# Short weight subtractions beside indirect writes, index products on VectorE, index copies on ScalarE, another pace of the list writes

## The chip, the cores and the metric

The kernel runs on one core of a Trainium2 chip. The metric is the device time of one execution in microseconds. Engines are called as in the profile: PE (TensorE), ACT (ScalarE), DVE (VectorE), POOL (GpSimd) and SP (the queue that issues most transfers).

## The reference, cut to what matters

Two transformer blocks over 256 tokens of width 2048. The stage that is changed is the feed-forward part of the first block, a retrieval over 16,384 one-neuron experts:

```python
q = einsum('td,de->te', ht, w_q)                          # 8 heads x 2 halves x 128
scores = einsum('thcd,hcnd->thcn', q, sub_keys)
s1, i1 = top_k(scores[:, :, 0], 16)
s2, i2 = top_k(scores[:, :, 1], 16)
cand_scores = s1[..., :, None] + s2[..., None, :]         # 16 x 16 for each head
cand_idx = i1[..., :, None] * 128 + i2[..., None, :]
top_scores, top_pos = top_k(cand_scores, 16)
experts = take_along_axis(cand_idx, top_pos)              # 128 experts for each token
gates = softmax(top_scores)
a = einsum('td,thkd->thk', x, u[experts])
out = einsum('thk,thkd->td', gates * gelu(a), v[experts])
```

## The kernel before

The tokens are two tiles (tt = 0 and 1) of 128. Every large product goes through PE in pieces: one piece is a weight block of 128 x 4 x 512 values, read into `raw` (3 buffers), copied by ACT into `whi` in a shorter format (L155), and the rest `wlo = raw - whi` taken by DVE (L156). PE then makes 24 matmuls of 512 columns (L180 to L182: hi x hi, hi x lo, lo x hi, for four rows of the block and two token tiles). `whi` and `wlo` have 3 buffers each, and `split(i + AHEAD)` with AHEAD = 2 stands ahead of the matmuls of piece i. So the split of piece i + 2 can start when PE has ended piece i - 1, and PE needs it when it comes to piece i + 2.

All other work is written as generators, in a list `tasks`. After the matmuls of each piece, `tick()` steps every generator once, in the order in which they were spawned. What a step issues stands in the engines' queues behind the split of that tick and ahead of the next one. Each queue is worked off in order, so a `yield` more or less moves all that follows by one piece. Nothing else orders the work.

The generators in this stage, in order of time:

- `peer_q(c)`, four chunks of four pieces (one per 512 columns of the query product), gives scores; `lists` takes the 16 best of 128 for each half head by `top16`: two maxima, two index searches, one replacement, and a cast of the indices from integers (L929).
- `route`, spawned ahead of all of them, works through the 8 heads of tile 0 and then of tile 1: candidates (L944), `top16` over 256, and for each pair of heads a position split into row and column (L954 to L957), one-hot masks (L960), their product with the index tables on POOL (L964), and a sum on DVE (L969). At its end come the softmax (its exponential on ACT, L974) and the expert numbers. `lists` for tile 1 is called from here. While tile 1 is routed, the gates of tile 0 are being written.
- `scatter_gates(tt)`: in each of 32 ticks DVE makes four comparisons (L1021), and POOL issues four indirect writes of 128 values each (L1006) into a table `gm` in memory, 128 writes for a tile. The table's 128 x 16,384 places say which expert has which gate. The next tile's writes start when those of the tile before are issued.
- `find_hits(tt)` reads the table back in 16 reads of 512 KB and reduces each (L1043); SP holds a read until all writes of the tile have landed.
- `list_experts` numbers the experts that were hit and issues 128 more indirect writes (`ls`, L1006); then SP reads the list back (L1136) and DVE copies it (L1139). With it the second half, `expert_v`, gathers its rows.

Meanwhile PE goes through the 32 chunks of `expert_u`, four pieces each; after the first piece of a chunk it transposes the chunk before (L235, eight transposes), ACT applies gelu to them (L1156), and ahead of that ACT has emptied the accumulators (L1150). Eight pieces of `mem_kv` follow, then 111 pieces of `expert_v`.

Of the kernel before, what the change touches and what calls it, by code (L numbers as in the profile page):

```python
# [8 lines left out]
F = mybir.dt.float32  # L9
# [5 lines left out]
OP = mybir.AluOpType  # L15
# [23 lines left out]
def tile_kernel(ctx, tc, a, o):  # L39
# [11 lines left out]
    def new(shape, dt=F, cls=None):  # L51
        n = 4 if dt != B16 else 2
        for s in shape[1:]:
            n *= s
        if cls is None:
            cls = next(c for c in SIZES if SIZES[c] >= n)
        uid[0] += 1
        return ar.tile(list(shape), dt, tag=cls, bufs=SLOTS[cls], name=f"{cls}_{uid[0]}")
# [32 lines left out]
    def spawn(gen):  # L91
        t = Task(gen)
        tasks.append(t)
        return t
# [32 lines left out]
    def load_raw(i):  # L127

        if i < len(srcs):
# [14 lines left out]
                    load(t[:, k], ap[:, k])  # L144
            raws[i] = t

    def split(i):
        if i < len(srcs):
            kt, n = srcs[i][1:3]
            live[home(i)].remove(i)  # L150
            r = raws.pop(i)
            hi = wp.tile([P, kt, n], R, tag="whi", bufs=SPLIT_BUFS, name=f"whi{i}")
            lo = wp.tile([P, kt, n], R, tag="wlo", bufs=SPLIT_BUFS, name=f"wlo{i}")
            for k in parts(i, kt):
                S.copy(hi[:, k], r[:, k])  # L155
                V.tensor_sub(lo[:, k], r[:, k], hi[:, k].bitcast(F))  # L156
            splits[i] = (hi, lo)

    def nxt():
# [754 lines left out]
    def lists(c, tt, sc):  # L914
        for b in range(4):
            top16(slot["s"][:, tt, 4 * c + b], slot["i"][:, tt, 4 * c + b], sc[:, b], P)
            if b % 2:
                yield

    def top16(val, idx, src, n):  # L920

        iu = new([P, 16], U32)
        rest = new([P, n])
        V.max(val[:, 0:8], src)
        V.max_index(iu[:, 0:8], val[:, 0:8], src)
        V.match_replace(rest, val[:, 0:8], src, -3.0e38)
        V.max(val[:, 8:16], rest)
        V.max_index(iu[:, 8:16], val[:, 8:16], rest)
        V.tensor_copy(idx, iu)  # L929

    def route():

        for tt in range(2):
            s, ix = slot["s"][:, tt], slot["i"][:, tt]
            ts, tp = new([P, 8, 16]), new([P, 8, 16])
            hi, lo = new([P, 8, 16]), new([P, 8, 16])
            i16 = st["iota"][:, :16]
            for h in range(8):
                while ("pq", h // 2) not in st or not st["pq", h // 2].done:
                    yield  # L940
                if tt and h % 2 == 0:
                    yield from lists(h // 2, 1, st["scores", h // 4][:, h // 2 % 2])
                cand = new([P, 16, 16])
                V.tensor_tensor(cand, s[:, 2 * h].unsqueeze(2).to_broadcast([P, 16, 16]),  # L944
                                s[:, 2 * h + 1].unsqueeze(1).to_broadcast([P, 16, 16]), op=OP.add)
                top16(ts[:, h], tp[:, h], cand.rearrange("p a b -> p (a b)"), 256)
                if tt:
                    yield
                if h % 2 == 0:
                    yield  # L950
                    continue

                h0, hs = h - 1, slice(h - 1, h + 1)
                V.tensor_scalar(hi[:, hs], tp[:, hs], 1.0 / 16, -0.46875, op0=OP.mult, op1=OP.add)  # L954
                V.tensor_scalar(hi[:, hs], hi[:, hs], 12582912.0, None, op0=OP.add)
                V.tensor_scalar(hi[:, hs], hi[:, hs], 12582912.0, None, op0=OP.subtract)
                V.scalar_tensor_tensor(lo[:, hs], hi[:, hs], -16.0, tp[:, hs], op0=OP.mult, op1=OP.add)  # L957
                eqs = [new([P, 2, 16, 16], cls="k2") for _ in range(2)]
                for eq, sel in zip(eqs, (hi, lo)):
                    V.tensor_tensor(eq, sel[:, hs].unsqueeze(3).to_broadcast([P, 2, 16, 16]),  # L960
                                    i16.unsqueeze(1).unsqueeze(1).to_broadcast([P, 2, 16, 16]), op=OP.is_equal)
                src = ix.rearrange("p (h c) k -> p h c k", c=2)[:, hs]
                for which, eq in enumerate(eqs):
                    G.tensor_tensor(eq, eq, src[:, :, which].unsqueeze(2).to_broadcast([P, 2, 16, 16]), op=OP.mult)  # L964
                yield
                if tt:
                    yield
                for eq, nm in zip(eqs, ("i1", "i2")):
                    V.tensor_reduce(slot[nm][:, tt, 16 * h0:16 * h0 + 32].rearrange("p (h k) -> p h k", h=2), eq,  # L969
                                    axis=AX.X, op=OP.add)  # L970
            nm8, sm = new([P, 8]), new([P, 8])
            V.tensor_scalar(nm8, ts[:, :, 0], -1.0, None, op0=OP.mult)
            V.tensor_tensor(ts, ts, nm8.unsqueeze(2).to_broadcast([P, 8, 16]), op=OP.add)
            S.activation(ts, ts, AF.Exp)  # L974
            V.tensor_reduce(sm, ts, axis=AX.X, op=OP.add)
            V.reciprocal(sm, sm)
            V.tensor_tensor(slot["gt"][:, tt].rearrange("p (h k) -> p h k", h=8), ts,
                            sm.unsqueeze(2).to_broadcast([P, 8, 16]), op=OP.mult)
            if tt == 0:
                slot["ex"], slot["au"] = new([P, 2, 2, P]), new([P, 2, P], U32)  # L980
            ex, au, ad = slot["ex"][:, tt, 0], slot["au"][:, tt], new([P, P])
            V.scalar_tensor_tensor(ex, slot["i1"][:, tt], float(P), slot["i2"][:, tt], op0=OP.mult, op1=OP.add)
            V.tensor_scalar(ad, ex, float(P), st["token"], op0=OP.mult, op1=OP.add)


            eh, ah = (x.rearrange("p (h k) -> p h k", h=8) for x in (ex, ad))
            eq, twice = new([P, 7, 7, 7], cls="k2"), new([P, 7, 7])
            V.tensor_tensor(eq, eh[:, 1:8, 0:7].unsqueeze(3).to_broadcast([P, 7, 7, 7]),
                            eh[:, 0:7, 9:16].unsqueeze(2).to_broadcast([P, 7, 7, 7]), op=OP.is_equal)
            V.tensor_reduce(twice, eq, axis=AX.X, op=OP.max)  # L990
            V.scalar_tensor_tensor(ah[:, 1:8, 0:7], twice, float(1 << 22), ah[:, 1:8, 0:7], op0=OP.mult, op1=OP.add)
            V.tensor_copy(au, ad)
            st["scatter", tt] = spawn(scatter_gates(tt, ex, au, slot["ex"][:, tt, 1]))
            yield
        while not st["scatter", 1].done:
            yield
        st["list"] = spawn(list_experts())
# [15 lines left out]
    def scatter_gates(tt, ex, au, total):  # L1013

        while tt and not st["scatter", 0].done:
            yield
        gt, group = slot["gt"][:, tt], []
        for k0 in range(0, P, 4):
            for k in range(k0, k0 + 4):
                same = new([P, P])  # L1020
                V.scalar_tensor_tensor(same, ex, ex[:, k:k + 1], gt, op0=OP.is_equal, op1=OP.mult, accum_out=total[:, k:k + 1])  # L1021
            for k in range(k0, k0 + 4):
                group.append(scatter("gates%d" % tt, gm[tt], au[:, k:k + 1], total[:, k:k + 1], group[k - 8:k - 7] if k >= 8 else ()))
            yield
        st["group", tt] = group
        if tt == 0:
            st["hits"] = new([P, 2, P])
            spawn(find_hits(0, 1))

    def find_hits(tt, pace):  # L1030

        for _ in range(3):
            yield
        ready.append(tt)
        pend = []
        for d in range(16 + 2 * pace):
            if d < 16:
                gt = new([P, 8, P])
                after_all(nc.sync.dma_start(gt, gmp[tt][d]).ins, st["group", tt])
                pend.append(gt)  # L1040
            if d >= 2 * pace:
                e = d - 2 * pace
                V.tensor_reduce(st["hits"][:, tt, 8 * e:8 * e + 8], pend[e], axis=AX.X, op=OP.max)  # L1043
            if d % pace == pace - 1:
                yield
        st["factors", tt] = spawn(early_factors(tt))
# [24 lines left out]

    def list_experts():

        yield from find_hits(1, 2)
        hits = st["hits"]

        cat, catT, num = new([P, 3, P]), new([P, 3, P]), new([P, 4])
# [51 lines left out]
        group = []  # L1129
        for k in range(P):  # L1130
            group.append(scatter("list", ls, pu[:, k:k + 1], ids[:, k:k + 1]))
            if k % 9 in (4, 8):
                yield
        yield
        lt = new([P, P])
        after_all(nc.sync.dma_start(lt, lsr).ins, group)  # L1136
        yield
# [666 lines left out]
```

## Time and profile before

| what | value |
|---|---|
| median of 3 runs | 3247.7 us (3247.1 to 3254.99) |
| the profiled execution | 3245.81 us, its span 3244.0 us |
| mean granted TensorE clock | 0.986 of full speed |
| busy: PE, DVE, ACT, POOL | 3129.6, 1932.4, 1494.0, 1087.8 us |
| PE without work from 939 to 1242 us | 26.6 us |
| PE without work from 1476 to 1542 us | 13.6 us |
| PE without work from 1735 to 1779 us | 33.8 us |

The profiled execution is 1.9 us below the median of the runs, and 1.8 us of it lie outside the span. Times in the rows below count from the start of the span. "Granted clock" is the share of full speed that the throttle left to PE. A row of the timeline has start, duration, engine, line, operation, output and inputs, and in brackets how long the engine had been idle and who released it.

### The profile page before, as it was taken

Reading aid. Unit: us, or ns where it says so; the run is one execution under the profiler, and the core shown is the slowest. Engines: PE = TensorE matmul, PEld = TensorE weight load, DVE = VectorE, ACT = ScalarE, POOL = GpSimd, SP = SyncE. Lnnn points to the kernel's source line nnn. Section 1 sums busy time; section 2 is a strip of 40 time slices with the busy share of each in tenths; the row PEclk is TensorE's granted clock in tenths of the full one; section 3 lists DMA queues with packets and bytes.
Section 4 is the critical chain, followed back from the end, with each engine's and each line's share of the span. In section 5 each row is a group of like instructions: output and inputs, shape, how many; then the busy total and the mean of one; then the engine's idle time right before and its main releaser. Section 6 shows DMA issues by size and latency. Waiting matters only on the chain. (4 is left out here: it accounts for less than half of the span.)

```text
span 3244.0 us, 38522 instructions
## 1 busy us (share of the span) xinstructions
PE 3129.6 (96%) x14755; PEld 2583.1 (80%) x14755; DVE 1932.4 (60%) x2445; ACT 1494.0 (46%) x1755; POOL 1087.8 (34%) x798
## 2 busy tenths in 40 slices
PE   8999999999999899998995999999999999999998
PEld 7888888888887777886884788888888888888886
DVE  5544555555579876765642466666765546665545
ACT  6566565433444334443442455555534544444442
POOL 1211131000002888881786388765000002000001
PEclk9999999999999999999997999999999999999999
DMA  7676455555545556897994677888744456644454
GB/s 259 207 259 213 159 191 190 189 209 209 213 170 174 184 188 225 297 317 291 351 314 141 226 293 289 293 286 285 253 151 167 149 207 233 217 159 165 143 209 154
DMA packets 169486, 715.97 MB, mean 221 GB/s; under 512 B 28769, under 2 KB 63010, under 8 KB 100946
## 3 DMA queue, kind: packets, MB, share of 16 engines
q1 hardware_dynamic: 135378, 581.99, 51.4%
q0 software_dynamic: 33920, 131.47, 11.6%
q8 instruction: 118, 1.93, 0.2%
q14 instruction: 70, 0.57, 0.0%
HBM read 658.59 MB, written 54.79 MB: 220 GB/s over the span
## 5 line engine op out<-in xcount | busy, mean ns | idle before, releaser
L156 DVE TENSOR_TENSOR wlo<-raw,whi 128x2048 fp32r<-128x2048 f32 (+3 forms) x521 | 1165.2, 2239 | 851.5 <-ACT whi L155 816.3
L181 PE MATMUL acc<-wlo,k 128*128 128x512 f32 (+3 forms) x3540 | 1367.3, 386 | 69.1 <-DVE wlo L156 52.9
L180 PE MATMUL acc<-whi,k 128*128 128x512 f32 (+3 forms) x3540 | 1395.5, 394 | 15.7 <-ACT whi L155 15.7
L182 PE MATMUL acc<-whi,k 128*128 128x512 f32 (+3 forms) x3540 | 1373.0, 388 | 0.0
L155 ACT CAST whi<-raw 128x2048 fp32r<-128x2048 f32 (+3 forms) x521 | 963.5, 1851 | 726.6 <-PE acc L182 411.8
L181 PEld LDWEIGHTS acc<-wlo,k 128*128 128x128 f32 x3540 | 668.6, 189 | 211.4 <-DVE wlo L156 59.3
L182 PEld LDWEIGHTS acc<-whi,k 128*128 128x128 f32 x3540 | 668.1, 189 | 144.4
L180 PEld LDWEIGHTS acc<-whi,k 128*128 128x128 f32 x3540 | 668.9, 189 | 143.4 <-ACT whi L155 16.1
L1006 POOL DMA_INDIRECT gm<-k,k x256 | 353.4, 1380 | 88.4 <-issue 45.2
L1006 POOL DMA_INDIRECT ls<-b,b x128 | 170.3, 1330 | 110.5 <-DVE b L1120 72.0
L1198 POOL DMA_INDIRECT k<-wd,b x111 | 174.3, 1570 | 34.5 <-issue 34.5
L223 POOL TENSOR_SCALAR b<-b 128x8 f32<-128x8 f32 (+1 forms) x22 | 6.9, 314 | 481.4 <-ACT b L257 241.3
L1532 POOL TENSOR_TENSOR k<-k,k 128x1024 f32<-128x1024 f32 x8 | 19.2, 2406 | 369.8 <-ACT k L1531 328.8
L1198 POOL DMA_INDIRECT raw<-peer_v_dram,b x73 | 101.8, 1394 | 99.9 <-DVE wlo L156 76.2
L1278 PE MATMUL acc<-whi,k 128*128 128x512 f32 x324 | 127.6, 394 | 3.0 <-DVEq L1233 3.0
L1279 PE MATMUL acc<-wlo,k 128*128 128x512 f32 x324 | 127.6, 394 | 0.0
L156 DVE TENSOR_TENSOR wlo<-k,whi 128x2048 fp32r<-128x2048 f32 x38 | 87.1, 2292 | 61.2 <-ACT whi L155 61.2
L235 PE MATMUL bt<-ident,k 128*128 128x128 f32 x800 | 109.3, 276 | 6.3 <-DVE k L244 3.5
L235 PEld LDWEIGHTS bt<-ident,k 128*128 128x128 f32 x800 | 93.9, 141 | 22.6 <-DVE k L244 4.9
L155 ACT CAST whi<-k 128x2048 fp32r<-128x2048 f32 x38 | 72.4, 1904 | 77.9 <-PE bs L1281 74.5
L775 POOL TENSOR_TENSOR k<-k,k 128x1024 f32<-128x1024 f32 x8 | 19.4, 2420 | 262.4 <-ACT k L774 262.4
L1429 POOL COPY b<-k 128x128 f32<-128x128 f32 x4 | 8.9, 2224 | 273.1 <-DVE k L1427 273.1
(366 smaller groups left out, 2789.3 us busy)
## 6 DMA issues: line engine op xcount, KB each, us to landing
raw<-w_dram SPq DMA_DIRECT2D x176, 1024.0 KB
raw<-peer_u_dram SPq DMA_DIRECT2D x128, 1024.0 KB
raw<-w_out_dram SPq DMA_DIRECT2D x64, 1024.0 KB
gm<-k SPq DMA_DIRECT2D x32, 512.0 KB
raw<-w_peer_q_dram SPq DMA_DIRECT2D x16, 1024.0 KB
wd<-k SPq DMA_DIRECT2D x32, 512.0 KB
k<-gm SPq DMA_DIRECT2D x32, 512.0 KB
k<-gm SPq DMA_DIRECT2D x64, 256.0 KB
```

The lines of the kernel that those rows point to most:

```text
L155: S.copy(hi[:, k], r[:, k])
L156: V.tensor_sub(lo[:, k], r[:, k], hi[:, k].bitcast(F))
L180: PE.matmul(out, xh, wh, start=first, stop=False)
L181: PE.matmul(out, xh, wl, start=False, stop=False)
L182: PE.matmul(out, xl, wh, start=False, stop=last)
L235: PE.transpose(pt[:, b, tt * P:(tt + 1) * P], ins[b0 + b][tt], ident)
L775: G.tensor_tensor(z, z, y, op=OP.mult)
L1006: ins = G.indirect_dma_start(dst, bass.IndirectOffsetOnAxis(ap=idx, axis=0), src, None, bounds_check=dst.shape[0] - 1, oob_is_err=False).ins
L1198: G.indirect_dma_start(dst, None, src, bass.IndirectOffsetOnAxis(ap=idx, axis=0), bounds_check=src.shape[0] - 1, oob_is_err=True)
L1278: PE.matmul(acc[n], h, hi[:, n], start=first, stop=False)
L1279: PE.matmul(acc[n], h, lo[:, n], start=False, stop=False)
L1532: G.tensor_tensor(z, z, y.rearrange("p a h d -> p a (h d)"), op=OP.mult)
```

## The change

Five edits. While `short` is set, from the spawn of tile 0's gate writes to the end of the list writes, the subtraction of a piece is made as four of 128 x 512 instead of one of 128 x 2048. The cast of the indices in `top16` goes from DVE to ACT (for both tiles, 48 casts). For tile 1 the product of masks and index tables goes from POOL to DVE; `lists` for tile 1 yields after each of its four calls instead of after two, and one yield behind the product falls away. `find_hits` waits two ticks instead of three, and for tile 1 handles three reads in a tick instead of two. The list writes are issued four in a tick instead of four and five by turns.

```diff
--- before.py
+++ after.py
@@ -144,6 +144,8 @@
                     load(t[:, k], ap[:, k])
             raws[i] = t
 
+    short = [False]
+
     def split(i):
         if i < len(srcs):
             kt, n = srcs[i][1:3]
@@ -153,7 +155,8 @@
             lo = wp.tile([P, kt, n], R, tag="wlo", bufs=SPLIT_BUFS, name=f"wlo{i}")
             for k in parts(i, kt):
                 S.copy(hi[:, k], r[:, k])
-                V.tensor_sub(lo[:, k], r[:, k], hi[:, k].bitcast(F))
+                for j in range(k.start, k.stop) if short[0] else (k,):
+                    V.tensor_sub(lo[:, j], r[:, j], hi[:, j].bitcast(F))
             splits[i] = (hi, lo)
 
     def nxt():
@@ -914,7 +917,7 @@
     def lists(c, tt, sc):
         for b in range(4):
             top16(slot["s"][:, tt, 4 * c + b], slot["i"][:, tt, 4 * c + b], sc[:, b], P)
-            if b % 2:
+            if b % 2 or tt:
                 yield
 
     def top16(val, idx, src, n):
@@ -926,7 +929,7 @@
         V.match_replace(rest, val[:, 0:8], src, -3.0e38)
         V.max(val[:, 8:16], rest)
         V.max_index(iu[:, 8:16], val[:, 8:16], rest)
-        V.tensor_copy(idx, iu)
+        S.copy(idx, iu)
 
     def route():
 
@@ -961,10 +964,9 @@
                                     i16.unsqueeze(1).unsqueeze(1).to_broadcast([P, 2, 16, 16]), op=OP.is_equal)
                 src = ix.rearrange("p (h c) k -> p h c k", c=2)[:, hs]
                 for which, eq in enumerate(eqs):
-                    G.tensor_tensor(eq, eq, src[:, :, which].unsqueeze(2).to_broadcast([P, 2, 16, 16]), op=OP.mult)
-                yield
-                if tt:
-                    yield
+
+                    (V if tt else G).tensor_tensor(eq, eq, src[:, :, which].unsqueeze(2).to_broadcast([P, 2, 16, 16]), op=OP.mult)
+                yield
                 for eq, nm in zip(eqs, ("i1", "i2")):
                     V.tensor_reduce(slot[nm][:, tt, 16 * h0:16 * h0 + 32].rearrange("p (h k) -> p h k", h=2), eq,
                                     axis=AX.X, op=OP.add)
@@ -991,6 +993,7 @@
             V.scalar_tensor_tensor(ah[:, 1:8, 0:7], twice, float(1 << 22), ah[:, 1:8, 0:7], op0=OP.mult, op1=OP.add)
             V.tensor_copy(au, ad)
             st["scatter", tt] = spawn(scatter_gates(tt, ex, au, slot["ex"][:, tt, 1]))
+            short[0] = True
             yield
         while not st["scatter", 1].done:
             yield
@@ -1029,7 +1032,7 @@
 
     def find_hits(tt, pace):
 
-        for _ in range(3):
+        for _ in range(2):
             yield
         ready.append(tt)
         pend = []
@@ -1071,7 +1074,7 @@
 
     def list_experts():
 
-        yield from find_hits(1, 2)
+        yield from find_hits(1, 3)
         hits = st["hits"]
 
         cat, catT, num = new([P, 3, P]), new([P, 3, P]), new([P, 4])
@@ -1129,9 +1132,10 @@
         group = []
         for k in range(P):
             group.append(scatter("list", ls, pu[:, k:k + 1], ids[:, k:k + 1]))
-            if k % 9 in (4, 8):
+            if k % 4 == 3:
                 yield
         yield
+        short[0] = False
         lt = new([P, P])
         after_all(nc.sync.dma_start(lt, lsr).ins, group)
         yield
```

What stands in the queues, at three places. In the rows a tile has its pool's name and running numbers; `x4` behind a row counts equal ones in a row.

ACT, tile 0's routing, the ticks of one pair of heads in the middle of `peer_q`. Before (`raw`/`whi` are a piece's blocks, L896 and L907 empty transposes and scores, L890 the accumulators):

```order
L155 CAST whi_6899<-raw_6761 128x2048
...
L155 CAST whi_6941<-raw_6805 128x2048
L907 COPY k_687_6986<-bs_6981 128x512
L907 COPY k_668_6799<-bs_6988 128x512
L155 CAST whi_6994<-raw_6851 128x2048
L155 CAST whi_7060<-raw_6903 128x2048
L890 ACTIVATE k_698_7090<-acc_6897,rh 128x512
L890 ACTIVATE k_698_7090<-acc_6898,rh 128x512
```

The same place in the changed kernel, where L932 is the cast of the indices:

```order
L157 CAST whi_6941<-raw_6805 128x2048
L932 CAST b_656_6616<-b_684_6973 128x16
L910 COPY k_687_6986<-bs_6981 128x512
L910 COPY k_668_6799<-bs_6988 128x512
L157 CAST whi_6994<-raw_6851 128x2048
L932 CAST b_656_6616<-b_690_7026 128x16
L932 CAST k_646_6552<-b_694_7044 128x16
L932 CAST k_646_6552<-b_696_7052 128x16
L157 CAST whi_7060<-raw_6903 128x2048
L893 ACTIVATE k_698_7090<-acc_6897,rh 128x512
L893 ACTIVATE k_698_7090<-acc_6898,rh 128x512
L932 CAST k_646_6552<-b_700_7096 128x16
```

One to three casts that read what DVE has just made now stand between one piece's `whi` and the next one's.

DVE, tile 1's routing, from the masks (L960) to their sums (L969). Before:

```order
L960 TENSOR_TENSOR k_879_8547<-b_781_7768,iota 128x512
L1021 SCALAR_TENSOR_TENSOR b_880_8552,k_771_7722<-k_771_7722,k_647_6553 128x128
...
L156 TENSOR_TENSOR wlo_8585<-raw_8399,whi_8584 128x2048
L1021 SCALAR_TENSOR_TENSOR b_886_8614,k_771_7722<-k_771_7722,k_647_6553 128x128
...
L156 TENSOR_TENSOR wlo_8635<-raw_8450,whi_8634 128x2048
L969 TENSOR_REDUCE k_647_6553<-k_878_8546 128x32
L969 TENSOR_REDUCE k_647_6553<-k_879_8547 128x32
```

In the changed kernel (L963 the masks, L968 the products, L971 the sums):

```order
L963 TENSOR_TENSOR k_895_8762<-b_781_7771,iota 128x512
L968 TENSOR_TENSOR k_894_8761<-k_894_8761,k_646_6552 128x512
L968 TENSOR_TENSOR k_895_8762<-k_895_8762,k_646_6552 128x512
L1024 SCALAR_TENSOR_TENSOR b_896_8767,k_771_7722<-k_771_7722,k_647_6553 128x128
...
L159 TENSOR_TENSOR wlo_8790<-raw_8610,whi_8789 128x512 x4
L971 TENSOR_REDUCE k_647_6553<-k_894_8761 128x32
L971 TENSOR_REDUCE k_647_6553<-k_895_8762 128x32
```

The products stand on DVE itself, one tick lies between masks and sums instead of two, and the subtraction is four rows.

POOL, the same stretch of the kernel before, where the products stand between the indirect writes of tile 0's gates:

```order
L964 TENSOR_TENSOR k_878_8546<-k_878_8546,k_646_6552 128x512
L964 TENSOR_TENSOR k_879_8547<-k_879_8547,k_646_6552 128x512
L1006 DMA gm_75<-k_771_7722,k_772_7723 2097152x1 x28
L964 TENSOR_TENSOR k_932_8996<-k_932_8996,k_646_6552 128x512
L964 TENSOR_TENSOR k_933_8997<-k_933_8997,k_646_6552 128x512
```

In the changed kernel the last product on POOL belongs to tile 0, and all writes follow each other.

By ticks the changed queues stand so: four ticks more for tile 1's routing (eight for a pair of heads instead of seven), so that tile 1's gate writes end one tick later; the first reduction of tile 1's table in the same tick as before; the first list write three ticks earlier; the copy of the list on DVE one tick later.

## Rows read from the trace of the kernel before

**Rows 1.** The page, part 1: busy time, share of the span, instructions.
```profile
PE 3129.6 (96%) x14755; PEld 2583.1 (80%) x14755; DVE 1932.4 (60%) x2445; ACT 1494.0 (46%) x1755; POOL 1087.8 (34%) x798
```

**Rows 2.** Busy time by stretch, then granted clock, DMA share, GB/s.
```profile
1029.00:1242.00 213.00, 188.50 (x818) 151.53 (x817) 174.01 (x566) 82.17 (x69) 171.47 (x124) 0.94 0.54 179
1476.00:1542.00 66.00, 52.38 (x234) 41.71 (x233) 46.22 (x38) 24.54 (x20) 0.94 (x1) 0.92 0.95 363
```

**Rows 3.** Timeline of PE: the transposes that each chunk makes once.
```profile
974.43 1.03 PE L235 MATMUL bt<-ident,k 128*128 128x128 f32 x8
999.09 1.04 PE L235 MATMUL bt<-ident,k 128*128 128x128 f32 x8
...
1241.23 1.03 PE L235 MATMUL bt<-ident,k 128*128 128x128 f32 x8
...
1469.87 1.03 PE L235 MATMUL bt<-ident,k 128*128 128x128 f32 x8
...
1558.01 1.03 PE L235 MATMUL bt<-ident,k 128*128 128x128 f32 x8
...
1718.06 1.03 PE L235 MATMUL bt<-ident,k 128*128 128x128 f32 x8
1777.67 1.04 PE L235 MATMUL bt<-ident,k 128*128 128x128 f32 x8
```

**Rows 4.** Groups by line, DVE, 939 to 1242 us: busy, mean ns, idle before.
```profile
L156 DVE TENSOR_TENSOR wlo<-raw,whi 128x2048 fp32r<-128x2048 f32 x46 | 106.1, 2312 | 2.7 <-issue 2.4 <-ACT whi L155 0.2
...
L969 DVE TENSOR_REDUCE k<-k 128x32 f32<-128x512 f32 x16 | 10.7, 682 | 32.1 <-POOL k L964 32.1
```

**Rows 5.** Timeline of DVE, tile 0's routing.
```profile
961.66 2.29 DVE L156 TENSOR_TENSOR wlo<-raw,whi 128x2048 fp32r<-128x2048 f32 x1
...
987.43 2.29 DVE L156 TENSOR_TENSOR wlo<-raw,whi 128x2048 fp32r<-128x2048 f32 x1
...
1003.96 0.17 DVE L929 CAST k<-b 128x16 f32<-128x16 uint32 x1
```

**Rows 6.** Timeline of DVE, tile 1's routing.
```profile
1061.72 1.28 DVE L960 TENSOR_TENSOR k<-b,iota 128x512 f32<-128x512 f32 x2
...
1107.63 2.28 DVE L156 TENSOR_TENSOR wlo<-raw,whi 128x2048 fp32r<-128x2048 f32 x1
...
1110.92 2.28 DVE L156 TENSOR_TENSOR wlo<-raw,whi 128x2048 fp32r<-128x2048 f32 x1
...
1128.29 2.33 DVE L156 TENSOR_TENSOR wlo<-raw,whi 128x2048 fp32r<-128x2048 f32 x1
...
1170.47 0.69 DVE L969 TENSOR_REDUCE k<-k 128x32 f32<-128x512 f32 x1 [8.60 <-POOL k L964]
...
1176.97 2.34 DVE L156 TENSOR_TENSOR wlo<-raw,whi 128x2048 fp32r<-128x2048 f32 x1
```

**Rows 7.** Timelines of ACT and PE at the end of tile 1's routing.
```profile
1221.54 0.31 ACT L974 ACTIVATE b<-b 128x128 f32<-128x128 f32 x1 [12.88 <-DVE b L973]
...
1224.13 5.50 ACT L155 CAST whi<-raw 128x2048 fp32r<-128x2048 f32 x3
...
1226.09 0.80 PE L180 MATMUL acc<-whi,k 128*128 128x512 f32 x1 [3.88 <-ACT whi L155]
```

**Rows 8.** Timelines of POOL and DVE: indirect writes beside DVE's work.
```profile
1555.23 2.29 DVE L156 TENSOR_TENSOR wlo<-raw,whi 128x2048 fp32r<-128x2048 f32 x1 [2.24 <-ACT whi L155]
...
1555.42 2.95 POOL L1006 DMA_INDIRECT ls<-b,b  x1 [0.30 <-issue]
...
1062.21 1.05 POOL L1006 DMA_INDIRECT gm<-k,k  x1 [0.30 <-issue]
```

**Rows 9.** Timelines: first and last of 128 list writes, the list's copy.
```profile
1548.96 1.17 POOL L1006 DMA_INDIRECT ls<-b,b  x1 [72.02 <-DVE b L1120]
...
1761.58 0.97 POOL L1006 DMA_INDIRECT ls<-b,b  x1 [0.30 <-issue]
...
1765.51 0.23 DVE L1139 CAST b<-b 128x128 uint32<-128x128 f32 x1 [41.62 <-DMA b<-ls]
```

## Prediction

> **What bounds the kernel now.** I read the page first: PE is busy for 96% of the span [rows 1], so a change to other engines can win only where PE waits. The transposes that PE makes once per chunk are a ruler for that. Undisturbed chunks are 22.86 us apart: ten lie between 1241.23 and 1469.87, seven between 1558.01 and 1718.06 [rows 3]. Three stretches are longer. The nine chunks from 999.09 to 1241.23 take 242.1 us where 205.7 would do: **36.4 us lost**, the routing. The three from 1469.87 to 1558.01 take 88.1 instead of 68.6: **19.5 lost**, the gate read-back. The one from 1718.06 to 1777.67 takes 59.6: **36.7 lost**, the list. Each loss is PE's idle time plus a remainder at a lower clock. In 1029 to 1242 PE is busy for 188.5 of 213 us, and the granted clock is 0.94, a mixture of 1.2 and 2.4 GHz [rows 2].
>
> Then I asked who makes PE wait. In the routing it is DVE: in 303 us its 46 subtractions found the engine idle for only 2.7 us, while the sums L969 waited 32.1 us for POOL's products [rows 4], up to 8.60 us at once [rows 6]. In the gates, POOL is still at the last write of tile 1 at 1476 (one instruction, 0.94 us, in the stretch from there [rows 2]), so the read-back, DVE's reductions and the next `wlo` are late. In the list the copy L1139 waits 41.62 us on DVE, from 1723.9, because the last of 128 writes ends at 1762.6 [rows 9]; the next `wlo` stands behind it, and PE uses up some 5 us of lead before it stops.
>
> **Tile 1's products on DVE, two yields fewer, four ticks more.** From one pair of heads to the next DVE takes 1176.97 - 1128.29 = 48.7 us [rows 6] for seven pieces, and PE would need 7 x 22.86 / 4 = 40.0. In the changed order a pair has eight ticks, 45.7 us for PE. DVE's work: 48.7, less 8.6 and about 0.5 for the two waits on POOL, is 39.6; two products at the mask's price, 1.28 for a pair, bring 1.3; a tick more has a subtraction and four comparisons, 1110.92 - 1107.63 = 3.3; six casts fewer save 0.2 each (0.17 busy [rows 5]), 1.2 together. No row before has a row of four short subtractions. Two masks of 128 x 512 take 1.28 [rows 6], so I take 0.61 each, 2.4 for four, where one long one takes 2.2 to the start of the next: 0.2 a tick, 1.8 in eight. The lower bound is 0, the upper the whole 0.64 each, 0.36 a tick. Sum 44.8, under PE's 45.7. With this alone the loss of 36.4 would go.
>
> **The casts on ACT.** ACT has time (46% busy), but its queue is in order. A cast of indices reads what DVE's last search has just made, and the next `whi` stands behind it. In a tick that ends with a `top16`, `whi` can no longer be ready in advance: after the search come the cast and `whi`, and only then the subtraction. The trace has one case of this: the exponential L974 waits 12.88 us for DVE, three `whi` stand behind it and run together for 5.50 us, and PE waits 3.88 us for `whi` [rows 7]. No row has the cast itself; the nearest on ACT is that exponential, 0.31 for 128 x 128, and I take 0.2. With `whi` at 1.83 (5.50 / 3) the detour costs DVE 2.1 us, less what else DVE has to do behind the search. Its lower bound is nothing, where DVE is early enough that `whi` waits for PE anyway; that is so only while DVE does not lag, and in this stretch it lags.
>
> Tile 0: a pair takes DVE 987.43 - 961.66 = 25.8 us [rows 5], PE's four pieces of the query product 24.7 (974.43 to 999.09 [rows 3]). Six casts off save 1.2; three of four ticks end with a search: 3 x 2.1 = 6.3; 0.3 for the round trip ahead of L954, which reads a cast at once; 1 for the score copies that follow a cast on ACT. Sum 32.2, 7.5 too long. Three pairs: the first uses up the lead (some 4 us lost), then 7.5 and 8.5: **20 us**, where before it was 2.
>
> Tile 1: six of eight ticks end with a search, but four comparisons (1.1) follow, so 1.0 each, and in two of them gelu (about 1) stands on ACT as well: 44.8 + 8 = 52.8 against 45.7, 7.1 a pair, four pairs: **28 us**. Some 20 short stops with a little clock after each: 5 us. Routing after: 20 + 28 + 5 = 53, against 36.4: **+17 us**. The bounds are -36 (the casts cost nothing) and +30 (DVE's lag never shrinks).
>
> **Short subtractions beside indirect writes.** A write that starts inside a subtraction does not end until 0.85 us after it: 1555.42 + 2.95 against 1555.23 + 2.29. Undisturbed it takes 0.97, with 0.30 ahead of it [rows 8, 9], so four need 5.1 us of a tick's 5.7. The first long subtraction in a tick thus costs POOL up to 2.2 us, 1.6 on average: the list took 213.6 us (1548.96 to 1762.6), which is 49.8 over 128 x 1.28 and falls on the 31 subtractions before 1723.9. Between two masks back to back a write gets through: begun at 1062.21 inside the first, it takes 1.05 and ends 0.3 us after the second, not 0.85 [rows 6, 8]. So a write is held for the rest of one short subtraction, 0.3 on average; with two starts in 2.4 us, 0.6 a tick. The Trainium skill (SBUF — State Buffer, Who interferes with whom) says that a DVE instruction with two SBUF inputs contends only with a GpSimd instruction that reads SBUF, and infers that descriptor generation is spared; by that rule this part gains nothing and the sum would be +17. The rows above contradict it.
>
> **List.** The copy comes 35 ticks after the first write instead of 31, 200 us instead of 175. Needed: 163.8 + 35 x 0.65 + 3 for the read-back = 190. The copy finds its data; I leave 1.7 for stragglers: **-35**. SP's reads of `raw` behind L1136 are freed with it.
>
> **Gates.** Tile 1's writes now nearly keep pace with DVE and end about one tick after it, four ticks ahead of the first read; the wait goes. Some 2.5 of the 19.5 are the list's own matmuls and stay. New is the burst: 16 reads of 512 KB in six ticks with six `raw` of 1 MB, 14.7 MB in all. At the 363 GB/s of the same place before [rows 2] that is 40 us in 34. I charge 5 us (0 to 17, all that was to be won): **-12**. Tile 0's read-back, a tick earlier, I cost at nothing: its writes are paced by DVE, and PE has no late work there in ten chunks [rows 3]; without that cover SP would hold the next `raw` behind the first read, for one write or two.
>
> **Sum.** +17 - 35 - 12 = -30: the profiled 3245.8 becomes 3216, and the median of the runs, 1.9 above it, 3218. I take **3217**; the likeliest case's own range is 3203 to 3232.
>
> **The rivals.**
> - *The port stays shut through all four short subtractions* (slower). For it: no row shows four; against it: the pair of masks. A write then waits 1.7 us a tick, and the list needs 163.8 + 35 x 1.75 + 3 = 228 of 200; DVE waits 28 less 5 of lead, so 22 to 23 are lost and only 14 won. Tile 1's writes end a tick later against the same first read: +6, and the burst +5. Sum +17 - 14 + 11 = +14: **3261**. It decides from 0.95 us a tick on, where the list begins to wait.
> - *The casts cost nothing on ACT.* The Trainium skill (Perfetto Trace Analysis, Optimizing Scalar/DVE Operations) says that work may well go to the scalar engine where DVE is saturated. As a mechanism here: `whi` would have to be early all the same. Both tiles then fit (24.9 for 24.7, 44.8 for 45.7), the routing's 36.4 go too: -36 - 35 - 12 = -83, **3165**. Rows 7 speak against it.
> - *The burst takes back the gates*: PE waits for reads instead of writes, 17 us: **3230**. The DMA share of 0.95 [rows 2] speaks for it, PE's lead of two pieces against it.
>
> **Chances.** Forecast 0.53; port shut 0.12; casts free 0.12; burst 0.18; something else 0.05, split evenly. 0.3% is 10 us and about what a measurement of this kernel can tell from no change. Faster by more than that: nearly all of the forecast's (0.52), casts free 0.12, most of the burst's 0.13: 0.77. Within it 0.12, slower 0.11, mainly the port. Range 3184 to 3252: it leaves out the free casts (0.12) and the upper half of the port case (0.08).
>
> **What would show it.** Right: L969's successor waits for nothing; ACT idles for DVE ahead of the index casts; DVE's idle time ahead of the subtraction is put down to `whi` all through the routing, with many PE gaps of 1 to 3 us; no idle time over 5 us at the list's copy; indirect writes mostly near 1 to 1.5 us. Wrong: PE without gaps in the routing (the casts are free), writes of 3 us beside the short subtractions (the port), or DVE waiting for reads of `gm` by more than a piece. If the routing loses over 83 us, the whole sign turns.

## Result and the profile after

The changed kernel took **3211.85 us** in the median of 4 runs (3208.4 to 3219.8), the one before 3247.4 beside it: ratio 0.989, 95% interval 0.987 to 0.991, faster by 35.5 us. Predicted were 3217. The profiled execution is the longest of the four (3219.75, span 3218.0); its extra 8 us lie behind 1789 us, in a part that the change does not touch. A later batch gave no gain; it stands at the end of the experiments. Here and below a time is the median of the runs within 1.5% of the kernel's fastest; the twelve that this leaves out, up to 3349.5 us, are all of kernels with short subtractions on the two chips of the later batches.

The ruler of [rows 3], PE's transposes (line L238 now; L183 to L185 are the matmuls, L157 `whi`, L159 `wlo`, L932 the cast of indices, L1143 the list's copy), in PE's timeline after:

```profile
925.99 1.03 PE L238 MATMUL bt<-ident,k 128*128 128x128 f32 x8
...
983.22 2.33 PE L238 MATMUL bt<-ident,k 128*128 128x128 f32 x8 [4.87 <-ACT k L893]
1015.27 2.33 PE L238 MATMUL bt<-ident,k 128*128 128x128 f32 x8 [4.68 <-ACT k L1154]
...
1283.41 1.03 PE L238 MATMUL bt<-ident,k 128*128 128x128 f32 x8
...
1512.05 1.03 PE L238 MATMUL bt<-ident,k 128*128 128x128 f32 x8
1537.28 1.03 PE L238 MATMUL bt<-ident,k 128*128 128x128 f32 x8
...
1765.91 1.04 PE L238 MATMUL bt<-ident,k 128*128 128x128 f32 x8
```

The thirteen chunks from 925.99 to 1283.41 take 357.4 us. Undisturbed they would take 3 x 24.66 (the query products, [rows 3]) + 10 x 22.86 = 302.6, so the routing loses **54.8** where it lost 36.4. From there to 1512.05 are ten chunks of 22.86; the chunk with the list's own matmuls takes 25.23, so the gates lose **2.4** instead of 19.5; from 1537.28 to 1765.91 are again ten of 22.86, and the list loses **nothing** instead of 36.7. Together +18.4 - 17.1 - 36.7 = -35.4, which is the difference of the medians.

The stretches of the routing, of the ten chunks behind it, of the gates and of the list (columns as in [rows 2]):

```profile
939.00:1284.00 345.00, 312.89 (x1338) 246.93 (x1337) 279.58 (x900) 135.26 (x154) 162.82 (x143) 0.96 0.50 167
1284.00:1512.00 228.00, 228.00 (x1037) 187.99 (x1035) 175.10 (x435) 98.88 (x80) 139.47 (x122) 1.00 0.93 326
1512.00:1561.00 49.00, 49.00 (x239) 40.87 (x237) 36.99 (x73) 20.09 (x17) 22.74 (x19) 1.00 0.95 340
1561.00:1766.00 205.00, 205.00 (x931) 168.94 (x930) 111.39 (x149) 92.48 (x76) 140.29 (x114) 1.00 0.89 299
```

Only in the routing is PE idle at all (312.89 of 345), with DVE idle there too (279.58, 81%): neither engine is the bound, they wait for each other. The waits of 939 to 1284 us say over which engine:

```profile
ACT k L932 <- DVE b L931: 108.9, 28, 9.1
...
ACT b L932 <- DVE b L931: 84.7, 15, 7.1
DVE wlo L159 <- ACT whi L157: 59.3, 37, 3.4
...
PE acc L183 <- ACT whi L157: 12.4, 9, 2.3
...
PE bt L238 <- ACT k L1154: 6.5, 7, 4.7
...
PE bt L238 <- ACT k L893: 5.4, 3, 4.9
```

One turn of that circle, ACT's and then DVE's timeline in tile 0:

```profile
989.27 0.20 ACT L932 CAST k<-b 128x16 f32<-128x16 uint32 x1 [1.36 <-DVE b L931]
989.38 1.91 ACT L157 CAST whi<-raw 128x2048 fp32r<-128x2048 f32 x1
```
```profile
988.96 0.29 DVE L931 FIND_INDEX8 b<-k,b 128x8 uint32<-128x128 f32 x1
991.32 2.29 DVE L159 TENSOR_TENSOR wlo<-raw,whi 128x2048 fp32r<-128x2048 f32 x1 [2.08 <-ACT whi L157]
```

The search ends at 989.25, the cast takes 0.20, `whi` starts only behind it, and DVE stands idle for 2.08 us: the detour priced at 2.1. Before, DVE's 46 subtractions had found 2.7 us of idle time in all [rows 4].

The list: POOL's first and last write, then DVE's copy, which waited 41.62 us in [rows 9].

```profile
1532.78 1.17 POOL L1009 DMA_INDIRECT ls<-b,b  x1 [72.44 <-DVE b L1123]
...
1725.65 1.49 POOL L1009 DMA_INDIRECT ls<-b,b  x1 [0.30 <-issue]
...
1734.56 0.23 DVE L1143 CAST b<-b 128x128 uint32<-128x128 f32 x1 [3.51 <-DMA b<-ls]
```

The 128 writes took 194.4 us instead of 213.6, and the copy stands 201.8 us behind the first of them. It still waited 3.51 us: its data came 7.4 us after the last write's end (1727.14), where the kernel before took 2.95.

### The profile page after: what moved, and what is told of

Same layout as the page of the kernel before. It is cut to its first block, busy times and chain, and to the rows that moved or that the text cites. A ratio compares the mean times of both kernels' runs of the same rounds, so it can differ in the third digit from the quotient of the medians.

```text
span 3218.0 us, 38917 instructions
## 1 busy us (share of the span) xinstructions
PE 3143.6 (98%) x14755; PEld 2584.3 (80%) x14755; DVE 1958.7 (61%) x2747; ACT 1498.6 (47%) x1803; POOL 1045.0 (32%) x790
## 3 DMA queue, kind: packets, MB, share of 16 engines
q0 software_dynamic: 33920, 131.47, 11.9%
## 5 line engine op out<-in xcount | busy, mean ns | idle before, releaser
L159 DVE TENSOR_TENSOR wlo<-raw,whi 128x512 fp32r<-128x512 f32 (+4 forms) x863 | 1193.2, 1416 | 890.2 <-ACT whi L157 889.4
L183 PE MATMUL acc<-whi,k 128*128 128x512 f32 (+3 forms) x3540 | 1396.3, 394 | 24.0 <-ACT whi L157 24.0
L185 PE MATMUL acc<-whi,k 128*128 128x512 f32 (+3 forms) x3540 | 1373.1, 388 | 0.0
L157 ACT CAST whi<-raw 128x2048 fp32r<-128x2048 f32 (+3 forms) x521 | 963.0, 1851 | 588.2 <-PE acc L185 349.7
L183 PEld LDWEIGHTS acc<-whi,k 128*128 128x128 f32 x3540 | 668.9, 189 | 156.0 <-ACT whi L157 29.1
L185 PEld LDWEIGHTS acc<-whi,k 128*128 128x128 f32 x3540 | 667.2, 188 | 144.4
L1009 POOL DMA_INDIRECT gm<-k,k x256 | 288.9, 1128 | 125.1 <-DVE b L1024 65.7
L1202 POOL DMA_INDIRECT k<-wd,b x111 | 193.5, 1744 | 34.7 <-issue 33.2
L1009 POOL DMA_INDIRECT ls<-b,b x128 | 151.1, 1180 | 110.9 <-DVE b L1123 72.4
L1202 POOL DMA_INDIRECT raw<-peer_v_dram,b x73 | 120.0, 1643 | 73.3 <-DVE wlo L159 45.9
L238 PE MATMUL bt<-ident,k 128*128 128x128 f32 x800 | 112.4, 278 | 18.7 <-ACT k L1154 6.5
L238 PEld LDWEIGHTS bt<-ident,k 128*128 128x128 f32 x800 | 93.8, 142 | 38.7 <-ACT k L1154 10.4
L159 DVE TENSOR_TENSOR wlo<-k,whi 128x2048 fp32r<-128x2048 f32 x38 | 87.1, 2292 | 59.9 <-ACT whi L157 59.9
L157 ACT CAST whi<-k 128x2048 fp32r<-128x2048 f32 x38 | 72.4, 1905 | 69.9 <-PE bs L1285 66.3
```

What stands on the lines that cost most here:

```text
L159: V.tensor_sub(lo[:, j], r[:, j], hi[:, j].bitcast(F))
L183: PE.matmul(out, xh, wh, start=first, stop=False)
L185: PE.matmul(out, xl, wh, start=False, stop=last)
L238: PE.transpose(pt[:, b, tt * P:(tt + 1) * P], ins[b0 + b][tt], ident)
L1009: ins = G.indirect_dma_start(dst, bass.IndirectOffsetOnAxis(ap=idx, axis=0), src, None, bounds_check=dst.shape[0] - 1, oob_is_err=False).ins
L1202: G.indirect_dma_start(dst, None, src, bass.IndirectOffsetOnAxis(ap=idx, axis=0), bounds_check=src.shape[0] - 1, oob_is_err=True)
```

## The experiments

The ruler gives, for each kernel whose chunks are not overlaid by the waits told of at the end, the losses in its profile (the routing always over the thirteen chunks from about 925 us, the gates with tile 0's read-back) and the median:

| kernel | routing | gates | list | time, us |
|---|---|---|---|---|
| before | 36.4 | 19.5 | 36.7 | 3247.4 |
| changed | 54.8 | 2.4 | 0 | 3211.9 |
| changed, casts on DVE | 2.6 | 2.4 | 0 | 3161.0 |
| changed, one long subtraction | 49.0 | 49.0 | 16.6 | 3270.7 |
| before, casts on ACT | 63.8 | 19.7 | 36.6 | 3276.0 |
| changed, old pace of the list | 55.0 | 2.4 | 11.5 | 3222.9 |
| before, products on DVE | 3.1 | 38.1 | 32.5 | 3227.8 |

From one kernel to another the sums of the losses differ by what the medians differ, to about 2 us.

**Casts back on DVE.**

```diff
-        S.copy(idx, iu)
+        V.tensor_copy(idx, iu)
```

> The changed kernel with one line put back: the index cast of every search on DVE again, instead of ACT. Mine (the casts on ACT tie ACT's weight copies to DVE's searches, and that is all that the routing loses): the 54.8 us that the routing stretch loses against the grid of 22.86 us per chunk fall to between 0 and 8, the waits of the weight subtraction for ACT's copy fall from 59 us to under 10, gates and list stay as they are; time 3157 to 3166. Rival A (DVE has too much work again once it takes the casts and tile 1's products): the routing loses 25 to 40 and the time is 3182 to 3197. Rival B (the casts cost nothing where they are, the clock or PE's own transposes lose the time): 3209 to 3216.

3161.0 us (ratio to before 0.974, 0.972 to 0.976). The stretch of the routing and its waits:

```profile
939.00:1212.00 273.00, 270.99 (x1248) 223.69 (x1247) 264.39 (x883) 121.31 (x101) 149.77 (x133) 1.00 0.59 195
```
```profile
ACT whi L157 <- PE acc L185: 46.0, 14, 4.5
```

DVE is busy for 97% and PE loses almost nothing: `whi` now waits mostly for PE (46.0 us, against 10.7 for DVE). Here a DVE that is nearly full was no reason to take work from it, as its order suited PE. In the changed kernel the casts cost 51 us.

**Casts on ACT in the kernel before**, the same line the other way round.

> The kernel before with one line changed: the index cast of every search on ACT. Mine: tile 0, which lost almost nothing, loses 12 to 20 us, tile 1 loses 8 to 18 more than its 30 or so; gates and list as before; time 3270 to 3285. Rival A (the casts take work from a DVE that is 95% busy in tile 0 and so help or cost nothing): 3235 to 3250. Rival B (the ACT casts cost only where DVE also has the products): about 3248 with tile 0 unchanged.

3276.0 (1.008, 1.007 to 1.010). The first four chunks take 116.4 us instead of 99.5 (tile 0: +16.9), the other nine lose 10.5 more. In its waits, 925 to 1292 us, DVE's wait for `whi` is as large as in the changed kernel, while the sums still wait for POOL, less than the 32.1 before:

```profile
DVE wlo L156 <- ACT whi L155: 62.0, 37, 3.4
...
DVE k L969 <- POOL k L964: 19.1, 7, 7.3
```

Tile 1 thus lost 10.5 us more, not tile 0's 16.9. I read that as two waits that lie side by side and are paid once; no run separates them.

**The casts on ACT, but a step later.** A cast goes into a list and ACT gets it at the next tick, when its search has long ended; four casts whose result is read in the same tick go to DVE.

```diff
     def tick():
+        while casts:
+            S.copy(*casts.pop(0))
...
-        S.copy(idx, iu)
+        if now:
+            V.tensor_copy(idx, iu)
+        else:
+            casts.append((idx, iu))
```

> The changed kernel with its casts still on ACT, but each handed out one step later, behind ACT's next weight copy and long after its search has ended (the four casts per tile-0 pair end that are needed in the same step, 4 of 48 with 128 columns, go to DVE). Mine (the loss is the in-order wait of ACT for DVE and of DVE for ACT, not the casts' own work): the routing's 54.8 us fall to 0 to 8, time 3157 to 3170. Rival (ACT's own time for casts, or its evacuations, is what is late): 35 us or more stay lost, 3195 to 3215.

> The same kernel as the one with the casts handed out a step later. Its first profile had 33 stretches in which TensorE waited 30 us in all for nothing that the profile shows, from 1053 us on, and none in tile 0's four chunks, which ran at 24.66 us each as before the change. If those waits were a disturbance of that measurement: none of them here, routing lost 0 to 8, time 3157 to 3175. If they belong to the kernel: again over 15 us of them, 3200 or more.

The times, 3233.5 and 3230.7, missed it, and so did the routing's losses, 24.5 and 21.3, by waits of another kind (below). Tile 0's four chunks, ahead of those, lost nothing in either run; in the second one:

```profile
925.60:1022.45 96.85, 96.85 (x465) 80.80 (x464) 83.77 (x217) 46.19 (x55) 11.38 (x8) 1.00 0.49 169
```

96.85 us, with PE busy throughout, against 116.4 with the casts in place. ACT still makes 20 of tile 0's 24 casts there. So it is not ACT's time for them that costs, but that they stood ahead of a `whi` and waited for DVE. For tile 1 the run is no proof, as its chunks hold such waits.

**One long subtraction.** `short` is never set.

> The changed kernel with the weight subtraction as one long instruction throughout; pacing, deeper reads, casts on ACT and products on DVE stay. Mine (the shared port held by long subtractions is what makes both rows of indirect writes late): the list writes last 213 us or more again and the chunk behind the list loses 12 to 22 us; the gates' chunk loses 15 to 24; the routing gains back about 3; time 3236 to 3255. Rival (the later copy and the deeper reads do it alone): the list loses 10 at most and the gates 5 at most; time 3205 to 3220.

3270.7 (1.008, 1.006 to 1.009), slower than before, and more than I expected: list and routing came as written, the gates lost 49.0 instead of 15 to 24. POOL's writes of the gate table by line (count, busy, mean ns), of the changed kernel and then of this one:

```profile
L1009 POOL DMA_INDIRECT gm<-k,k x256 | 288.9, 1128 | 125.1 <-DVE b L1024 65.7 <-issue 40.2 <-DMA gm<-k,k 7.3
```
```profile
L1008 POOL DMA_INDIRECT gm<-k,k x256 | 378.5, 1478 | 87.4 <-issue 39.9 <-DVE b L1023 28.0 <-DMA gm<-k,k 5.8
```

A write takes 0.35 us longer, 90 us over 256, and both read-backs, a tick earlier than before the change, now wait for it on DVE:

```profile
1297.57 1.22 DVE L1045 TENSOR_REDUCE k<-k 128x8 f32<-128x1024 f32 x1 [14.29 <-DMA k<-gm]
...
1516.28 3.73 DVE L1045 TENSOR_REDUCE k<-k 128x8 f32<-128x1024 f32 x3 [31.60 <-DMA k<-gm]
```

The first is tile 0's read-back. So the early read-back is safe only with the short subtractions. How much of the 49.0 comes from the earlier reads is not shown: the kernel with the products alone (below) keeps the old reads and loses 38.1 there, and no run has the earlier reads by themselves.

**The old pace of the list.**

```diff
-            if k % 4 == 3:
+            if k % 9 in (4, 8):
```

> The changed kernel with the list writes handed out five and four at a time as before, so that the copy of the list stands four steps (23 us) earlier; short subtractions stay. Mine (the writes need about 190 us in any case, and the copy then stands 177 to 180 us behind the first of them): the copy waits 8 to 18 us longer on DVE, of which the weight splits made ahead hide some 5; time 3214 to 3227. Rival (the writes go faster when more are handed out at once): the wait stays under 5 us and the time is 3209 to 3214.

3222.9 (0.993, 0.991 to 0.994). The writes take 191.4 us, the copy stands 23 us earlier against the first of them if nothing waits, and does wait:

```profile
1726.76 0.23 DVE L1143 CAST b<-b 128x128 uint32<-128x128 f32 x1 [18.95 <-DMA b<-ls]
```

15.4 us more than in the changed kernel; the chunk loses 11.5. Of the list's 36.7 us the short subtractions thus take about 25 and the later copy the rest; the later copy without them leaves 16.6.

**Products on DVE alone**, with tile 1's yields regrouped as in the change.

> The kernel before with tile 1's products on DVE and the steps of tile 1 regrouped with it; long subtractions, old pacing, casts on DVE. Mine (the 36.4 us of tile 1 are waits for POOL): the routing loses 0 to 6; gates lose 15 to 30 and the list 30 to 40 as before; time 3205 to 3225. Rival (DVE cannot hold casts and products without loss, or its products hold the port and make the gate writes later): routing 20 to 35 or gates over 40, time 3230 to 3255.

3227.8 (0.995, 0.993 to 0.996). The routing's loss is gone as expected, 36.4 to 3.1; but the gates lose 38.1, not 15 to 30. DVE there:

```profile
1257.74 1.22 DVE L1041 TENSOR_REDUCE k<-k 128x8 f32<-128x1024 f32 x1 [15.29 <-DMA k<-gm]
...
1474.39 1.22 DVE L1041 TENSOR_REDUCE k<-k 128x8 f32<-128x1024 f32 x1 [29.50 <-DMA k<-gm]
```

The first is tile 0's read-back, the second tile 1's, for which DVE waited 19.24 us before the change. The 256 writes take as long as before (1.396 us each, 1.380 before). What PE no longer waits for in the routing, it waits for behind it: 18.5 of the 33.3 us gained there are given back.

**Two subtractions of 1024 columns.**

```diff
-                for j in range(k.start, k.stop) if short[0] else (k,):
+                for j in (slice(0, 2), slice(2, 4)) if short[0] else (k,):
```

> The changed kernel with the weight subtraction as two instructions of 1024 columns instead of four of 512. Mine (an indirect write is held until the subtraction in which it starts has ended, so the hold goes with the length): the list writes last 199 to 206 us, the list's chunk loses 2 to 9, the gates' 5 to 20, the routing 2 less; time 3216 to 3240. Rival (one opening between instructions is enough): list and gates lose as little as with four, 3206 to 3215.

> The same kernel as the one with two subtractions of 1024 columns. Its first profile had 20 us of waits of TensorE for nothing that the profile shows. If they were a disturbance: as that run was to show, by the length of the hold 3214 to 3230 (gates lost only 2.4 in its first profile, so now the list alone, 2 to 9), by one opening 3206 to 3214. If they belong to the kernel: again over 10 us of them, 3230 or more.

The medians, 3246.5 and 3242.8, are overlaid by those waits as well. POOL's rows are not:

```profile
L1009 POOL DMA_INDIRECT gm<-k,k x256 | 289.0, 1129 | 134.6 <-DVE b L1024 70.5 <-issue 51.0 <-DVE wlo L159 11.0
L1009 POOL DMA_INDIRECT ls<-b,b x128 | 153.0, 1195 | 118.0 <-DVE b L1123 79.6 <-issue 38.4
```

1.129 and 1.195 us a write (1.143 and 1.191 in the repetition), against 1.128 and 1.180 with four pieces and 1.478 and 1.376 with one. The changed kernel with the same waits in it (below) has 1.128 and 1.182, so it is not they that make the writes short: halving is nearly all of it. My expectation that the hold goes with the length was wrong.

**Four short subtractions alone**, in the kernel before.

> The kernel before with the four short subtractions alone: old pacing, old reads, casts on DVE, products on POOL. Mine: gates lose 2 to 6 instead of 19.5, the list loses 10 to 14 instead of 36.7 (as with the old pacing in the changed kernel, 11.5), tile 1's routing loses 30 to 45 (DVE has half a us more per step, POOL's products wait less); time 3200 to 3220. Rival (without the products on DVE the port is still held or the routing gets worse by the longer subtractions): 3225 to 3245.

> The same kernel as the one with the four short subtractions alone. Its first profile had 36 us of waits of TensorE for nothing that the profile shows. If they were a disturbance: gates lose 2 to 6, the list 10 to 14, the routing 20 to 30 (by the quiet chunks of the first profile), time 3190 to 3215. If they belong to short subtractions beside POOL's writes: again over 15 us of them, 3220 or more.

Medians 3239.7 and 3238.3, overlaid. In the second profile the routing loses 20.1 (30 to 45 was expected at first), less than before although DVE has more to do, and the chunk with the list's matmuls 3.3; a write of the gate table takes 1.124 us. What the gates' read-backs and the list lose can't be read from it.

**Waits without a cause in the profile.** The kernels above ran on three chips: the four with the casts back, long subtractions, casts in the kernel before and old pace on one; later casts, short alone, products and halves on a second; the repetitions of these but the products, and the changed kernel once more, on a third. The chip of the changed kernel's first batch is not known.

> The changed kernel itself once more, beside the kernels with two subtractions of 1024 columns and with later casts, whose traces show 20 to 30 us of waits of TensorE for nothing that the profile shows and whose times spread over 50 to 120 us. If short subtractions beside POOL's writes bring such waits on some chips: here too, over 10 us of them, and a median of 3225 or more. If they come with the particular program: none here, and 3205 to 3220.

The changed kernel took 3249.9 on the third (3232.6 to 3265.2, 8 runs), before 3247.1 (3242.4 to 3256.4, 13 runs): ratio 1.001, 0.998 to 1.004, no gain. Its profiled execution, 3232.6, the fastest of its runs, has the same 54.8 us in the routing; what is new sits in three chunks, 10.7, 2.2 and 8.2 us. The first of them behind an undisturbed one, and pieces of PE's, POOL's and DVE's timelines in it:

```profile
1282.60:1305.45 22.85, 22.85 (x106) 18.86 (x104) 15.74 (x48) 9.87 (x8) 17.98 (x17) 1.00 0.97 355
1305.45:1338.97 33.52, 28.81 (x106) 21.28 (x105) 20.79 (x57) 9.77 (x8) 19.89 (x20) 0.85 0.54 184
```
```profile
1309.60 0.39 PE L185 MATMUL acc<-whi,k 128*128 128x512 f32 x1 [0.58 <-issue]
...
1316.68 0.59 PE L184 MATMUL acc<-wlo,k 128*128 128x512 f32 x1 [0.62 <-issue]
...
1318.76 0.59 PE L184 MATMUL acc<-wlo,k 128*128 128x512 f32 x1 [0.65 <-issue]
...
1325.45 0.39 PE L184 MATMUL acc<-wlo,k 128*128 128x512 f32 x1
```
```profile
1316.35 0.97 POOL L1009 DMA_INDIRECT gm<-k,k  x1 [0.30 <-issue]
1325.47 0.97 POOL L1009 DMA_INDIRECT gm<-k,k  x1 [8.15 <-DVE b L1024]
```
```profile
1322.42 2.50 DVE L159 TENSOR_TENSOR wlo<-raw,whi 128x512 fp32r<-128x512 f32 x4 [12.73 <-ACT whi L157]
```

In the middle of a piece, whose blocks were split long before, PE waits between single matmuls for nothing that the profile shows. The waits end 1.4 us after POOL's row of back-to-back writes. DVE is idle from 1309.7 to 1322.4, so none of its instructions holds PE in any of them but the first. The granted clock falls (0.85 in the chunk, a mixture of the levels 1.2 and 2.4 GHz), but behind the first waits: the matmul at 1309.60 still takes 0.39 us, that at 1316.68 takes 0.59, and at 1325 it is 0.39 again. Waits over 0.2 us that the profile puts down to nothing: none in the first profile of the changed kernel or in the four of the first chip (two of these have short subtractions); 20 to 39 in each of the seven profiles with short subtractions on the other two. One to six in each end within 0.1 us of an ACT or DVE instruction that may have been what PE waited for; the rest are 17 to 36, 10 to 36 us together, all of them between 1040 and 1760 us, while the gate table and the list are written. The kernel with the products alone, whose subtractions are long, kept its time on the second chip (3226.8 to 3230.1 in 4 runs; its one wait put down to nothing, 6.5 us, is that for the `wlo` behind DVE's 15.29, and the kernel before has four of 1.5 to 7.0 us ahead of `wlo` in the same way). The kernel before had medians of 3246 to 3247 in every batch.

## Why the prediction was right, and where not

- **Sum and sign**: -35.4 us against -30, by the terms that were forecast. It holds for the first batch; in the last, on the third chip, 3249.9 lies above the likeliest case's 3203 to 3232 and only just inside the range to 3252. No step of the prediction had such a case: neither the waits nor that the gain could go from one batch to another.
- **Routing, +17**: +18.4. Tile 0 lost 19.6 us in its four chunks (20 forecast), tile 1 35.3 (28 and 5 of clock). The mechanism is shown from both sides (casts back: -52 us of loss; casts alone: +27) and by its cure in tile 0. One way was missing: PE's own transposes wait up to 4.87 us for ACT's evacuations (L893, L1154), which stand behind casts as well; at 11.9 us in ten waits they cost PE as much as the 12.4 for `whi`. The total came out better than its parts: PE is idle for only 32.1 of the 54.8 us (345 less 312.89), and the other 22.7 it spends busy, at a mean granted clock of 0.96, where 5 were put down to the clock.
- **Products on DVE**: the loss of 36.4 goes with them, as the sum of 44.8 against 45.7 said. That POOL's writes would then be late was not in the prediction; in the changed kernel the short subtractions hide it.
- **Four short subtractions**: 0.60 us from start to start, 0.61 taken. They carry the change: without them the changed kernel is 59 us slower. The rival of the closed port falls. The Trainium skill (SBUF — State Buffer, Who interferes with whom) infers that descriptor generation is spared by a two-input DVE instruction. Here the write as a whole is not spared: 1.478 against 1.128 us a write, for the same work in other pieces. Whether it is the making of descriptors that waits, or POOL's reading of the write's inputs, no run separates.
- **List, -35**: -36.7, with less to spare than forecast. The writes took 194.4 us for 187 (the 190 less 3 for the read-back) and the read-back 7.4 for 3, so the data came at 201.8 instead of 190, and DVE, at the copy after 198.3, waited 3.51 us. PE's lead covered that; of the 18.95 us at the old pace it did not cover 11.5.
- **Gates, -12**: -17.1. The step that failed in size is the 5 us for the burst of 16 reads: DVE's reductions waited 0.78 and 0.16 us for reads, no more, with a DMA share of 0.95. Tile 0's read-back cost nothing, as priced, but only with the short subtractions (14.29 us of wait without them). How much of the -17.1 the earlier and denser reads bring, no run shows, as none lacks them alone.
- **Casts free** (the rival at 3165): wrong here. The Trainium skill (Perfetto Trace Analysis, Optimizing Scalar/DVE Operations) says that offloading work to the scalar engine may make sense where DVE is saturated. Here DVE at 97% with the casts gave 3161, and at 81% without them 3212. The rival's time was right for another kernel, the one that leaves the casts alone.

What stays open: why PE waits beside POOL's writes in the batches on two of three chips, and whether the 3161 us hold there. POOL's row of writes and PE's waits come together in the trace; which of them makes the other is not shown, since an idle DVE also lets POOL write faster. That it is the chip and not the hour was not tried either, as each chip stands for one stretch of time.

## What to carry to other kernels

Moving a small instruction to an idle engine puts it into that engine's order: if what stands behind it feeds the engine that was to be relieved, both wait for each other, and handing it out a step later takes the wait away. A gain ahead of a stream with its own length (here 256 writes) is in part given back behind it unless the stream gets shorter too, so edits that look separate have to be timed together. Repeat a gain of one per cent in another batch, on another chip if there is one, before believing it.

## What was not expected of the hardware

An indirect write profits from one opening in the subtraction almost as much as from three (1.129 and 1.128 us, 1.478 without). In the batches on two of three chips TensorE paused 0.2 to 2.4 us at a time between matmuls, 10 to 36 us in a profile, only in the stretch in which POOL writes the table and the list in kernels with short subtractions; the kernel before kept its time there.
